# The same decoder-layer program, its instructions ordered by the builder's plain rule instead of its simulated timeline

## The chip, the cores and the metric

The kernel runs on one core of one Trainium2 chip. Its time is the device time of one execution in microseconds (us); the number to be predicted is the median over undisturbed runs. The core has five instruction queues that the kernel fills: PE (TensorE, matmuls), DVE (VectorE), ACT (ScalarE), POOL (GpSimd) and SP (SyncE), and each works its queue off in order; DMA transfers are issued from SP, ACT and POOL and run beside them.

## What is computed

One decoder layer over 512 tokens of width 1024, all in float32: a norm, one input projection, a gated short convolution and a gated linear recurrence over chunks of 32 tokens, an output projection with its residual, then a PEER feed-forward layer and a last norm. The time goes to PEER:

```python
def peer_ffn(x, wq, keys, u_tab, v_tab):
    ...
    q = (xt @ wq).reshape(t, PEER_HEADS, 2, HALF_Q)
    scores = jnp.einsum('thpd,hpnd->thpn', q, keys).astype(jnp.float32)
    s_top, i_top = lax.top_k(scores, PEER_TOPK)
    cand = (s_top[:, :, 0, :, None] + s_top[:, :, 1, None, :]).reshape(t, PEER_HEADS, PEER_TOPK * PEER_TOPK)
    c_score, c_idx = lax.top_k(cand, PEER_TOPK)
    ...
    expert = i1 * N_KEYS + i2
    gates = jax.nn.softmax(c_score, axis=-1)
    ...
        u = jnp.take(u_tab, eb, axis=0)
        a = jax.nn.gelu(jnp.einsum('td,thkd->thk', xb, u).astype(jnp.float32), approximate=False)
        w = (gb * a).astype(xb.dtype)
        vv = jnp.take(v_tab, eb, axis=0)
        return jnp.einsum('thk,thkd->td', w, vv)
```

For each token and each of 8 heads, 16 of 16,384 experts are selected (128 per token), each with a row of 1024 numbers in a u table and one in a v table.

## The kernel before

The 512 tokens are four blocks of 128. Blocks 1 to 3 (384 tokens) do the feed-forward layer **densely**: all 16,384 experts in 128 chunks of 128, with the gates as a matrix that is zero where an expert is not selected. Block 0 does it **sparsely**: it gathers its 128 rows of u and 128 rows of v for all its tokens, one 512 KB gather per selected rank, and multiplies on DVE. So PE and DVE share the layer.

The stages, in the order of the program:

1. The front, to about 260 us: projections, convolution, recurrence, output projection, the norm before PEER (which writes h2, transposed by L469). Every float32 operand is split in two parts, hi (a rounded copy that ACT makes, L99, whi) and lo (what remains, that DVE makes, L101, wlo), and `mm3` multiplies in three passes, hi x hi, hi x lo, lo x hi, which are lines L115, L116 and L117 of every dense matmul.
2. Queries and scores, to about 360 us.
3. The u stage, to about 795 us: `uchunk(c)` loads a 128x1024 raw tile of u (SP queue), splits it (whi, wlo), runs 24 matmuls 128x384 into `pa` (two PSUM buffers), and ACT takes the gelu out of it (`gl`, L447); the first 84 chunks spill gl to DRAM. Beside them DVE selects the experts: the top 16 of the scores (L518 to L523), the candidates and their top 16 (L554 to L586), the look-up of the indices (L595 to L607), block 0's experts (L613). Then 24 times `gate_m` builds, with four DVE operations on 128x2048 tiles A and B (L644 to L647), 32 small matmuls (L656, L657) and ACT evictions (`stg`, L659), a part of the dense gate matrix, which goes to DRAM. From 439 us on POOL issues the gathers of block 0 (`rows`, L675): `gu(j)` multiplies a gathered u row with h2 on DVE (L681), 16 of them are followed by a gelu and the gate (L685), and `gv(j)` adds a gathered v row times its weight to y0 (L689).
4. The v stage, from about 795 us to the end: for each of 128 chunks `vchunk` loads a raw tile of v, splits it, multiplies gl with the gates (w, L744), splits that (wh on ACT L747, wl on DVE L749), and 18 matmuls 128x512 are added up in `y` (six PSUM banks). The first 41 v chunks alternate with the last 41 u chunks. The remaining gathers go on beside them, at a pace of 2.65 per pair of chunks, later 1.1 per v chunk.
5. The last norm of each block (`finish`, L799 to L807) and the output.

Raw tiles and gathered rows come from **one ring** of buffers (8 in the u stage, 12 in the v stage, `raw_ring`). The next tenant of a buffer may be loaded when DVE has done with the former one: for a raw tile that is its wlo (L101), for a gathered row its product (L681 or L689). whi and wlo have four buffers each. POOL issues the gathers in order, each when its buffer is free.

```python
    def split(src):
        hi = ws.tile([P, D], F32R, tag="hi", name="whi")
        S.activation(hi, src, AF.Copy)
        lo = ws.tile([P, D], F32R, tag="lo", name="wlo")
        V.tensor_sub(lo, src, hi.bitcast(F32))
        return hi, lo
```
```python
    def rows(tab, j):
        t = ring[0]()
        G.indirect_dma_start(out=t, out_offset=None, in_=a[tab],
                             in_offset=bass.IndirectOffsetOnAxis(ap=e_i32[:, j:j + 1], axis=0))
```

What sets the order: the program is written stage by stage, with gates, chunks and gathers interleaved by the counts above. The builder (`tile.TileContext`) records all instructions and then puts them in an order of its own, queue by queue, that keeps the dependencies; while it does so it hands out the ring buffers, so that a tile's address, too, is a result of the order. Before, it does so with `schedule_with_timeline_sim=True`: it simulates a timeline and lets its times decide what comes next.

## Time and profile before

| | us |
|---|---|
| median of 2 runs | 1502.42 (1502.3 to 1502.54) |
| the profiled execution | 1500.03 |
| its span in the trace | 1498.1 |
| PE busy | 1462.3 (98%) |
| DVE busy | 1201.3 (80%) |
| ACT busy | 637.0 (43%) |
| POOL busy | 365.8 (24%) |
| mean granted clock of PE | 0.99 |

The span is the time from the first to the last instruction in the trace; 1.9 us of the profiled execution lie around it. "Granted clock" is the share of TensorE's full clock that it was allowed. All times in the rows below count from the start of the span.

### The profile page before, as it was taken

What the parts mean: (1) busy time and instruction counts of PE and PEld (TensorE: products, weight loads), DVE (VectorE), ACT (ScalarE), POOL (GpSimd) and SP (SyncE); (2) the same over time, 40 slices, a digit from 0 to 9 for tenths busy, and PEclk for the clock granted to TensorE, in tenths of its full rate; (3) what the DMA queues carried; (4) which work ended last, traced back from release to release, by engine and by line L of the source; (5) the groups of instructions that cost most, each with busy time, mean ns of one, the idle gap of its engine ahead of it and who ended that gap; (6) DMA issues with size and microseconds to landing.
All of it is one profiled execution on the core that took longest, in us unless ns stands there. A gap on an engine that the chain in (4) does not pass through costs nothing.

```text
span 1498.1 us, 21741 instructions
## 1 busy us (share of the span) xinstructions
PE 1462.3 (98%) x7929; PEld 1297.3 (87%) x7929; DVE 1201.3 (80%) x2312; ACT 637.0 (43%) x900; POOL 365.8 (24%) x284
## 2 busy tenths in 40 slices
PE   7999999999998999999999999999999999999997
PEld 6887777888998998889999999999998888888886
DVE  5847876799989988788829878778787788888887
ACT  5833324333443365666744333333333333333333
POOL 0000000000034142320014445444343224333340
PEclk9999999999999999999999999999999999999999
DMA  6231233622469789689779999998989999999993
GB/s 230 85 106 43 70 127 112 246 86 90 161 209 386 244 279 315 231 293 321 261 287 419 324 337 323 338 341 313 345 298 338 368 369 368 355 356 352 352 342 118
DMA packets 137770, 394.64 MB, mean 263 GB/s; under 512 B 13120, under 2 KB 59584, under 8 KB 135488
## 3 DMA queue, kind: packets, MB, share of 16 engines
q1 hardware_dynamic: 47520, 170.94, 31.5%
q0 software_dynamic: 39168, 159.40, 29.4%
q10 hardware_dynamic: 50976, 62.93, 11.9%
q8 instruction: 62, 1.02, 0.3%
q14 instruction: 44, 0.36, 0.1%
HBM read 346.82 MB, written 46.40 MB: 262 GB/s over the span
## 4 chain that ended last, share of the span: by engine, by line
PE 76%; DVE 6%; ACT 5%; issue 5%; DMA 5%; POOL 2%; ACTq 1%; POOLq 0%; DVEq 0%
PE y L116 10%; PE y L115 10%; PE y L117 10%; PE pa L115 8%; PE pa L116 7%; PE pa L117 7%; PE pm L115 7%; PE pm L116 6%; PE pm L117 6%; ACT stg L659 4%; DMA wraw<-in_v_dram,e_i 2%; POOL wraw L675 2%; DVE wlo L101 2%; DMA wraw<-in_u_dram,e_i 1%; PE pm L538 1%
## 5 line engine op out<-in xcount | busy, mean ns | idle before, releaser
L99 ACT ACTIVATE whi<-wraw 128x1024 fp32r<-128x1024 f32 x308 | 325.8, 1058 | 518.4 <-PE pa L116 205.4
L101 DVE TENSOR_TENSOR wlo<-wraw,whi 128x1024 fp32r<-128x1024 f32 x308 | 376.2, 1222 | 144.8 <-ACT whi L99 141.1
L115 PE MATMUL pa<-h2Thi,whi 128*128 128x384 f32 x1024 | 348.0, 340 | 12.7 <-ACT gl L447 12.4
L117 PE MATMUL pa<-h2Thi,wlo 128*128 128x384 f32 x1024 | 346.6, 338 | 0.0
L116 PE MATMUL pa<-h2Tlo,whi 128*128 128x384 f32 x1024 | 346.2, 338 | 0.0
L675 POOL DMA_INDIRECT wraw<-in_u_dram,e_i x128 | 183.3, 1432 | 490.2 <-DVE ci L523 178.6
L116 PE MATMUL y<-wlo,wh 128*128 128x512 f32 x768 | 299.5, 390 | 0.0
L115 PE MATMUL y<-whi,wh 128*128 128x512 f32 x768 | 298.9, 389 | 0.2 <-ACT wh L747 0.2
L117 PE MATMUL y<-whi,wl 128*128 128x512 f32 x768 | 296.8, 390 | 0.0
L675 POOL DMA_INDIRECT wraw<-in_v_dram,e_i x128 | 169.4, 1323 | 263.2 <-DVE wlo L101 122.0
L115 PEld LDWEIGHTS pa<-h2Thi,whi 128*128 128x128 f32 x1024 | 194.3, 190 | 17.8 <-ACT gl L447 15.9
L116 PEld LDWEIGHTS pa<-h2Tlo,whi 128*128 128x128 f32 x1024 | 194.4, 190 | 1.6
L117 PEld LDWEIGHTS pa<-h2Thi,wlo 128*128 128x128 f32 x1024 | 194.1, 190 | 0.0
L681 DVE SCALAR_TENSOR_TENSOR wraw<-wraw,h2n 128x1024 f32<-128x1024 f32 x128 | 155.9, 1219 | 34.7 <-DMA wraw<-in_u_dram,e_i 34.6
L689 DVE SCALAR_TENSOR_TENSOR y<-wraw,w,y 128x1024 f32<-128x1024 f32 x128 | 163.9, 1280 | 17.1 <-DMA wraw<-in_v_dram,e_i 16.9
L117 PEld LDWEIGHTS y<-whi,wl 128*128 128x128 f32 x768 | 144.1, 188 | 30.2
L115 PEld LDWEIGHTS y<-whi,wh 128*128 128x128 f32 x768 | 144.2, 188 | 29.7 <-ACT wh L747 0.6
L116 PEld LDWEIGHTS y<-wlo,wh 128*128 128x128 f32 x768 | 144.1, 188 | 29.0
L747 ACT ACTIVATE wh<-w 128x384 fp32r<-128x384 f32 x128 | 65.8, 522 | 208.2 <-PE y L116 97.6
L659 ACT ACTIVATE stg<-pm 128x512 f32<-128x512 f32 x96 | 92.3, 1156 | 17.7 <-PE pm L657 17.7
L749 DVE TENSOR_TENSOR wl<-w,wh 128x384 fp32r<-128x384 f32 x128 | 70.2, 554 | 22.8 <-ACT wh L747 22.3
L115 PE MATMUL pm<-hThi,whi 128*128 128x512 f32 x192 | 77.7, 406 | 8.4 <-ACT whi L99 8.4
(240 smaller groups left out, 1694.7 us busy)
## 6 DMA issues: line engine op xcount, KB each, us to landing
wraw<-in_u_l_dram SPq DMA_DIRECT2D x128, 512.0 KB, 5.6
wraw<-in_v_l_dram SPq DMA_DIRECT2D x128, 512.0 KB, 6.4
Gd<-stg ACTq DMA_DIRECT2D x12, 2048.0 KB, 7.6
Gt<-Gd POOLq DMA_DIRECT2D x16, 1536.0 KB, 9.7
Ad<-gl ACTq DMA_DIRECT2D x84, 192.0 KB, 5.0
glr<-Ad ACTq DMA_DIRECT2D x84, 192.0 KB, 5.2
wraw<-in_w_in_dram SPq DMA_DIRECT2D x24, 512.0 KB, 3.7
wraw<-in_wq_dram SPq DMA_DIRECT2D x16, 512.0 KB, 7.4
```

What stands on the lines that cost most here:

```text
L99: S.activation(hi, src, AF.Copy)
L101: V.tensor_sub(lo, src, hi.bitcast(F32))
L115: PE.matmul(out, l[0], r[0], start=first, stop=False)
L116: PE.matmul(out, l[0], r[1], start=False, stop=False)
L117: PE.matmul(out, l[1], r[0], start=False, stop=last)
L538: PE.matmul(o[:, tb * NK:(tb + 1) * NK], q[:, tb * P:(tb + 1) * P], keys[:, i, :], start=True, stop=True)
L659: S.activation(st[:, t0:t0 + 4, :], o3, AF.Copy, scale=1.0 / GSC)
L675: G.indirect_dma_start(out=t, out_offset=None, in_=a[tab], in_offset=bass.IndirectOffsetOnAxis(ap=e_i32[:, j:j + 1], axis=0))
L681: V.scalar_tensor_tensor(r, r, 1.0, h2n, op0=OP.mult, op1=OP.mult, accum_out=act0[:, j:j + 1])
L689: V.scalar_tensor_tensor(y0, r, w0[:, j:j + 1], y0, op0=OP.mult, op1=OP.add)
L747: S.activation(wh, w, AF.Copy)
L749: V.tensor_sub(wl, w, wh.bitcast(F32))
```

## The change

One word in one line: the builder is told not to simulate a timeline, and orders the instructions by its plain rule.

```diff
-    with tile.TileContext(nc, schedule_with_timeline_sim=True) as tc, ExitStack() as ctx:
+    with tile.TileContext(nc, schedule_with_timeline_sim=False) as tc, ExitStack() as ctx:
```

The kernel's functions are untouched, and the instructions are the same (ACT's table loads apart, of which there are 19 instead of 21, since they depend on the order). What moves is shown at three places.

**DVE, u stage, at the first splits beside the selection.** In the names, wlo_3443, wlo_3477, wlo_3754 and wlo_3788 are the lo parts of four u chunks that follow one another; tv, ti, mr, cand, cv and ci belong to the selection. Before (19 rows of selection stand between the first two, 20 between the second and the third, 18 between the third and the fourth):

```order
L101 TENSOR_TENSOR wlo_3443<-wraw_3439,whi_3441 128x1024
L518 MAX tv1_2185<-s_3147 128x8
...
L523 MAX_INDEX ti3_2191<-tv3_2187,mr_3163 128x8
L101 TENSOR_TENSOR wlo_3477<-wraw_3473,whi_3475 128x1024
...
L522 MAX tv2_2186<-mr_3188 128x8
L101 TENSOR_TENSOR wlo_3754<-wraw_3750,whi_3752 128x1024
...
L558 TENSOR_TENSOR cand_3508<-tv1_2185 128x8x8
L101 TENSOR_TENSOR wlo_3788<-wraw_3784,whi_3786 128x1024
```

Of the change, the same stretch:

```order
L101 TENSOR_TENSOR wlo_3443<-wraw_3439,whi_3441 128x1024
L518 MAX tv1_2185<-s_3147 128x8
...
L522 MAX cv_3213<-mr_3259 128x8
L101 TENSOR_TENSOR wlo_3477<-wraw_3473,whi_3475 128x1024
...
L521 MATCH_REPLACE mr_3694<-cv_3648,cand_3640 128x50
L101 TENSOR_TENSOR wlo_3754<-wraw_3750,whi_3752 128x1024
L522 MAX cv_3648<-mr_3694 128x8
L101 TENSOR_TENSOR wlo_3788<-wraw_3784,whi_3786 128x1024
```

Now 87 rows stand between the first two and 197 between the second and the third (a row may stand for a few instructions of one form), and one between the third and the fourth. The selection moved ahead of wlo_3754.

**PE at the same place.** pa_3479 is the chunk of wlo_3477, pa_3756 that of wlo_3754, pa_3790 the next. Of the change, from the end of pa_3479 on (before, the first L117 of pa_3756 follows its first L115 and L116, and pa_3790 comes after it):

```order
L117 MATMUL pa_3479<-h2Thi_1870,wlo_3477 128x384
L115 MATMUL pa_3756<-h2Thi_1870,whi_3752 128x384
L116 MATMUL pa_3756<-h2Tlo_1871,whi_3752 128x384
L115 MATMUL pa_3790<-h2Thi_1870,whi_3786 128x384
L116 MATMUL pa_3790<-h2Tlo_1871,whi_3786 128x384
L117 MATMUL pa_3756<-h2Thi_1870,wlo_3754 128x384
```

Two matmuls of pa_3790 moved ahead; between the last matmul of the chunk before and the first that needs wlo_3754, four stand.

**DVE, v stage, around a gather.** wraw_11856 and wraw_11891 are gathered rows; the wlo are splits of raw tiles (wraw_11469 and so on); w and wl belong to v chunks. Before, from the product of the gathered row wraw_11821, which frees the buffer that wraw_11926 gets, to the product of that:

```order
L681 SCALAR_TENSOR_TENSOR wraw_11821,act0_2160<-wraw_11821,h2n_2162 128x1024
L749 TENSOR_TENSOR wl_11621<-w_11617,wh_11619 128x384
L744 TENSOR_TENSOR w_11760<-glr_11752,Gt_11215 128x384
L101 TENSOR_TENSOR wlo_11615<-wraw_11611,whi_11613 128x1024
L689 SCALAR_TENSOR_TENSOR y0_2163<-wraw_11856,w0_2161,y0_2163 128x1024
L749 TENSOR_TENSOR wl_11656<-w_11652,wh_11654 128x384
L101 TENSOR_TENSOR wlo_11650<-wraw_11646,whi_11648 128x1024
L681 SCALAR_TENSOR_TENSOR wraw_11891,act0_2160<-wraw_11891,h2n_2162 128x1024
L749 TENSOR_TENSOR wl_11694<-w_11690,wh_11692 128x384
L101 TENSOR_TENSOR wlo_11688<-wraw_11684,whi_11686 128x1024
L689 SCALAR_TENSOR_TENSOR y0_2163<-wraw_11926,w0_2161,y0_2163 128x1024
```

Of the change, from the split of wraw_11469, which frees the buffer that wraw_11856 gets:

```order
L101 TENSOR_TENSOR wlo_11473<-wraw_11469,whi_11471 128x1024
L681 SCALAR_TENSOR_TENSOR wraw_11821,act0_2160<-wraw_11821,h2n_2162 128x1024
L749 TENSOR_TENSOR wl_11516<-w_11512,wh_11514 128x384
L744 TENSOR_TENSOR w_11652<-glr_11644,Gt_11215 128x384
L101 TENSOR_TENSOR wlo_11510<-wraw_11506,whi_11508 128x1024
L689 SCALAR_TENSOR_TENSOR y0_2163<-wraw_11856,w0_2161,y0_2163 128x1024
L749 TENSOR_TENSOR wl_11551<-w_11547,wh_11549 128x384
L744 TENSOR_TENSOR w_11690<-glr_11682,Gt_11215 128x384
L101 TENSOR_TENSOR wlo_11545<-wraw_11541,whi_11543 128x1024
L681 SCALAR_TENSOR_TENSOR wraw_11891,act0_2160<-wraw_11891,h2n_2162 128x1024
```

The gathers moved about three chunks ahead against the splits, and each took over another buffer, as the addresses of the two built programs tell:

| gathered row | former tenant before | splits from its end to the use | former tenant in the change | splits from its end to the use |
|---|---|---|---|---|
| wraw_11821 | wraw_11714 | 3 | wraw_11434 | 1 |
| wraw_11856 | wraw_11749 | 4 | wraw_11469 | 1 |
| wraw_11891 | wraw_11784 | 3 | wraw_11506 | 1 |
| wraw_11926 | wraw_11821 | 3 | wraw_11541 | 1 |
| wraw_11961 | wraw_11856 | 3 | wraw_11576 | 1 |

Over the last 176 gathers (numbers 80 to 255) the splits from the freeing to the use are 1 for 10, 2 for 49, 3 for 67, 4 for 40 and 5 for 10 of them before; in the change 1 for 153, 2 for 22 and 3 for one.

In the u stage, besides, the 32 matmuls of a gate now stand together behind two chunks instead of among the matmuls of a chunk, six products of gathered rows (L681) stand in a row on DVE ahead of one of the first gates, and ACT's gl and stg copies stand there behind a whi. The three last `finish` stand one after another instead of interleaved.

## Rows read from the trace of the kernel before

**Rows 1.** The page's first table: busy time, share of the span, instructions.
```profile
PE 1462.3 (98%) x7929; PEld 1297.3 (87%) x7929; DVE 1201.3 (80%) x2312; ACT 637.0 (43%) x900; POOL 365.8 (24%) x284
```

**Rows 2.** A window: length, busy PE, PEld, DVE, ACT, POOL; clock; DMA share; GB/s.
```profile
1150.00:1200.00 50.00, 50.00 (x222) 41.42 (x221) 40.14 (x57) 17.64 (x25) 14.46 (x15) 1.00 0.98 366
```

**Rows 3.** Waits of PE: us in total, times, longest.
```profile
PE pa L115 <- ACT gl L447: 12.4, 8, 4.2
```

**Rows 4.** Windows as in rows 2, at two waits of PE.
```profile
455.00:460.00 5.00, 3.73 (x12) 3.73 (x13) 5.00 (x15) 1.70 (x3) 2.72 (x3) 0.50 0.98 349
...
590.00:595.00 5.00, 3.21 (x21) 2.89 (x21) 5.00 (x6) 1.44 (x2) 0.00 (x0) 1.00 1.06 388
```

**Rows 5.** PE's timeline there: start, length, instruction, idle before and its releaser.
```profile
456.27 0.69 PE L115 MATMUL pa<-h2Thi,whi 128*128 128x384 f32 x1 [4.17 <-ACT gl L447]
456.76 0.52 PE L116 MATMUL pa<-h2Tlo,whi 128*128 128x384 f32 x1
457.08 0.52 PE L117 MATMUL pa<-h2Thi,wlo 128*128 128x384 f32 x1
...
461.24 0.40 PE L115 MATMUL pa<-h2Thi,whi 128*128 128x384 f32 x1
...
593.51 0.40 PE L656 MATMUL pm<-B,A 128*128 128x128 f16 x4 [1.79 <-DVE B L646]
```

**Rows 6.** ACT's timeline, u stage: hi parts, released by finished chunks.
```profile
381.24 1.06 ACT L99 ACTIVATE whi<-wraw 128x1024 fp32r<-128x1024 f32 x1 [2.72 <-PE pa L116]
...
385.39 1.06 ACT L99 ACTIVATE whi<-wraw 128x1024 fp32r<-128x1024 f32 x1 [2.72 <-PE pa L116]
```

**Rows 7.** DVE's timeline at two of the splits (wlo_3443 and wlo_3754).
```profile
363.82 1.23 DVE L101 TENSOR_TENSOR wlo<-wraw,whi 128x1024 fp32r<-128x1024 f32 x1 [0.44 <-ACT whi L99]
...
374.54 1.21 DVE L101 TENSOR_TENSOR wlo<-wraw,whi 128x1024 fp32r<-128x1024 f32 x1
```

**Rows 8.** One window, DVE busy: all; L101 alone; L681 alone.
```profile
363.82:447.80 83.98, 79.52 (x435) 1.00 0.53 173
...
363.82:447.80 83.98, 21.82 (x18) 1.00 0.53 173
...
363.82:447.80 83.98, 7.33 (x12) 1.00 0.53 173
```

**Rows 9.** A window of PE alone: the u stage.
```profile
430.00:800.00 370.00, 355.19 (x2504) 0.98 0.84 295
```

**Rows 10.** Instruction groups of DVE: busy us, mean ns, idle before and releasers.
```profile
L101 DVE TENSOR_TENSOR wlo<-wraw,whi 128x1024 fp32r<-128x1024 f32 x308 | 376.2, 1222 | 144.8 <-ACT whi L99 141.1 <-PE pm L538 2.4
...
L689 DVE SCALAR_TENSOR_TENSOR y<-wraw,w,y 128x1024 f32<-128x1024 f32 x128 | 163.9, 1280 | 17.1 <-DMA wraw<-in_v_dram,e_i 16.9
...
L749 DVE TENSOR_TENSOR wl<-w,wh 128x384 fp32r<-128x384 f32 x128 | 70.2, 554 | 22.8 <-ACT wh L747 22.3
...
L744 DVE TENSOR_TENSOR w<-glr,Gt 128x384 f32<-128x384 f32 x84 | 43.0, 552 | 8.4 <-issue 5.3 <-DMA Gt<-Gd 2.8
```

**Rows 11.** Timelines of DVE and POOL: a buffer freed, the gather issued.
```profile
1013.90 1.23 DVE L101 TENSOR_TENSOR wlo<-wraw,whi 128x1024 fp32r<-128x1024 f32 x1 [2.32 <-ACT whi L99]
...
1015.40 1.01 POOL L675 DMA_INDIRECT wraw<-in_v_dram,e_i  x1 [3.00 <-DVE wlo L101]
```

**Rows 12.** The gathers' line (L675) by stretch: 550 to 750, 1130 to 1450.
```profile
DMA to landing us min/median/max: 4.9/5.9/12.6
...
DMA to landing us min/median/max: 4.5/7.3/13.9
```

**Rows 13.** The first of them as a window of POOL: busy, clock, DMA share, GB/s.
```profile
550.00:750.00 200.00, 41.66 (x18) 0.98 0.81 281
```

**Rows 14.** Waits of DVE from 795 to 1450 us.
```profile
DVE y L689 <- DMA wraw<-in_v_dram,e_i: 11.2, 13, 2.6
DVE wraw L681 <- DMA wraw<-in_u_dram,e_i: 10.4, 9, 2.5
```

**Rows 15.** DVE's timeline: its last instruction.
```profile
1493.52 1.41 DVE L806 SCALAR_TENSOR_TENSOR wraw<-wraw,vo,nfb 128x512 f32<-128x512 f32 x2
```

## The prediction

> **What bounds the kernel now.** I read the page's first table, the waits of the TensorE queue (PE), its busy time by stretches of 50 us, then the timelines where PE did wait. PE is busy for 1462.3 of 1498.1 us [rows 1]; VectorE (DVE), next, for 1201.3. From about 800 us, when the chunks of the v table run, a 50-us window is full: 50.00 us of PE, 41.42 in weight loads, DVE about 41 [rows 2]. So any order with the same instructions can gain at most the 36 us in which PE is idle, and loses every microsecond that it makes PE wait. The largest part of the idle time, 12.4 us, are eight waits of u chunks for the PSUM buffer that ACT's gelu frees [rows 3].
>
> PE's clock has a price of its own here. After the wait of 4.17 us that ended at 456.27 the window 455 to 460 ran at 0.50 (1.2 instead of 2.4 GHz); after the 1.79 us that ended at 593.51 the clock stayed 1.00 [rows 4, 5]. In the slow stretch a 384-column matmul starts every 0.32 us (456.76, 457.08) [rows 5]; at full clock a chunk's 24 take 4.15 us, 0.17 each [rows 6]. Over the 5 us from 456.27 to 461.24 that costs about 2.4, with its ends 3 us.
>
> **The change part by part.** No instruction is added or taken away apart from two table loads of ACT; the order in every queue changes, and with it which ring buffer each raw tile gets. I go through the program by stages. The first 360 us stand almost as they stood: 0 to +4, I take 0.
>
> *Selection ahead of the splits (360 to 450 us).* PE runs a u chunk each 4.15 us (381.24 to 385.39, the releases of ACT's whi by finished chunks) [rows 6]. Each needs a wlo from DVE. Before, DVE made wlo_3443 at 363.82, the one after next (wlo_3754) at 374.54 [rows 7], with a share of the selection between. Now all the selection instructions that the order shows between wlo_3443 and wlo_3754, 286 of them, come first. Their cost: DVE's busy time from 363.82 to 447.80 is 79.52; 21.82 of it are the splits and 7.33 six products of gathered rows, so selection is 79.52 - 21.82 - 7.33 = 50.4 us, nearly all of it now ahead of wlo_3754 [rows 8]. That split then ends at 363.8 + 1.2 + 50.4 + 2 x 1.2 = 417.8. Its chunk started at 385.4 before; two first matmuls of it and two of the next are all that PE has meanwhile. **+32 us** of idle PE, then half clock: **+3**. The order puts the next splits (wlo_3788, wlo_3822) right behind, so this is paid once. Nothing pays it back: PE has no slack later, and DVE's lead, gained by having selected early, is not what PE lacks. Bounds: 0, if the selection were spread after all, which the order excludes short of a wrong reading; 35, if all of it and the clock are paid.
>
> *Gates (430 to 800 us).* PE is busy 355.19 of these 370 us, so 14.8 idle plus some 6 of half clock are there to win [rows 9]. Against it, the 32 matmuls of a gate now stand together behind two chunks, and before one of the first gates stand six products of gathered rows on DVE, 7.3 us [rows 8] that PE waits for with its chunk splits behind it; ACT's gelu copies also stand behind a whi that waits for a gather's buffer. I take one such stall of 7.3 with its 3 of clock more than before: **+10**, bounds -15 (all of the idle time goes) and +20 (two).
>
> *The ring in the v stage (800 to 1450 us).* This is the largest term. A gather on POOL needs a ring buffer, which is free when DVE has done with its last tenant, and DVE waits in order for the landed rows. Before, 2 to 4 weight splits lie between the freeing and the use in three quarters of the cases; now just one in 153 of the last 176 gathers. Follow the rows of the change: wlo_11473 frees the buffer of wraw_11856; one split later DVE stands at its product and must wait until it is issued and landed; behind it come wl, w and the next wlo, which frees the next buffer but one. So two splits take R + 3.6 us, where R is from freeing to landing, and 3.6 is 1.28 + 0.55 + 0.55 + 1.22 [rows 10]. From freeing to issue takes 0.3 (a split ends at 1013.90 + 1.23 = 1015.13, POOL issues at 1015.40) [rows 11]. Landing is not one number: median 7.3 us from 1130 to 1450, where a window has 366 GB/s, and 5.9 from 550 to 750, at 281 GB/s [rows 2, 12, 13]. With slower chunks traffic thins: 366 x 4.1 / 4.9 is 306 GB/s, nearest to the second, so I take 5.9. R = 6.2, a split each (6.2 + 3.6) / 2 = 4.9 us against PE's 4.1 (18 matmuls; 222 in 50 us, some records missing [rows 2]). 0.8 x 169 splits (41 u and 128 v chunks) = 135; 23 of 176 gathers have a longer window, so 0.87 x 135: **+115**. Bounds: with the least landing shown, 4.5 [rows 12], it is (4.8 + 3.6) / 2 = 4.2, so +0 to 15; with 7.3 it is 5.6 and 1.5 x 169 = +250. DVE waited for landed rows only 11.2 + 10.4 us here before [rows 14]; covered by four split buffers, PE saw nothing of it.
>
> The Trainium skill, DMA: Bandwidth & Descriptors, section on the SWDGE path of one DMA, gives a fixed 2.0 us plus bytes over 436 GB/s for a transfer issued by GpSimd. For these 512 KB an estimate by it is 3.2 us, R = 3.5, a split each 3.6 us: PE would not wait and this term would be nothing (the first rival's 1550). The trace disagrees, with 4.5 as its least and 7.3 as its median.
>
> *Tail.* The three last norms stand one after another now; DVE's last instruction starts at 1493.52 and takes 1.41 [rows 15]; two more of these behind each other: **+3**, bounds 0 and 6.
>
> Sum on the profiled run of 1500.0: 1500 + 32 + 3 + 10 + 115 + 3 = 1663. The median of the runs shown is 2.4 above the profiled run (1502.42 against 1500.03), which gives **1665 us**.
>
> **The rivals.**
>
> *The gathers land in time.* As chunks slow down, landings fall to the least shown and the ring is no bound: 1665 - 115 = 1550. For it: traffic in the v stage is what lengthens the landings, and a ring that is waited for thins it. Against it: even at 281 GB/s the median is 5.9. It decides where R + 3.6 is under 2 x 4.1, a landing of 4.3.
>
> *The clock falls in the v stage too.* If the waits there bunch up to 3 us and more (landings reach 13.9 [rows 12]), each is followed by about 3 us lost. One such wait in every second of the 85 pairs of splits adds 42 x 3 = 126, in every pair 250: 1791 to 1915, say 1850. For it: a wait of 4.17 cost the clock. Against it: the mean wait is 1.6 per pair, and 1.79 did not [rows 4, 5]. The Trainium skill, TensorE: Matmul & The Clock Gate, in its section on HAM oscillation, tells of a kernel whose every step waits for a transfer and so starts each step at the low clock; the trace agrees for single long waits (0.50 after 4.17 us) and shows no such series.
>
> *Not slower.* The plain rule keeps PE's own queue dense and the waits of [rows 3] vanish: 12.4, 1.8 at the gate [rows 5] and 6 of clock, so 1502 - 20 = 1482. That holds if the selection block hides behind work of PE and the landings are 4.3 or less. For it: PE's matmuls are the same and its order is tighter. Against it: between the last matmul of one chunk and the first needing wlo_3754 only four matmuls, 0.7 us, stand. It ends on this side once that wait is under 20 us and the ring costs nothing.
>
> **How the numbers follow.** As forecast, with the ring at 4.7 to 5.6 a split: 0.70, own range 1600 to 1800. Gathers in time, about 1550: 0.12. Clock in the v stage, 1,800 and more: 0.13. Not slower: 0.05, 0.02 of it under 1472, the other 0.03 within 2%. The range 1545 to 1800 holds the first two, 0.82. About 2%, 30 us, is what a measurement of this kernel tells from no change: under 1472 faster (0.02), 1472 to 1532 the same (0.03), above it slower (0.95).
>
> **What would show it.** A PE wait of 30 us near 387 to 418, released by wlo of L101, then a clock of 0.50. In the v stage, waits of DVE's L681 and L689 for gathers of 100 us and more in sum, in place of 21.6; waits of PE's pa and y for wlo of about the sum forecast; splits 4.9 us apart; traffic near 306 GB/s; a landing near 5.9. No such wait near 400 would make the first term wrong. PE full after 800 would make the third wrong, by the landing if that is under 4.5, and by the reading of the ring if it isn't. A granted clock well under 1.00 there would speak for the second rival.

## The result, and the profile after

The median is 1731.99 us (1730.73 to 1733.25, two runs) against 1502.42: a ratio of 1.1531, 95% interval 1.1504 to 1.1559. The profiled execution has a span of 1729.0 us, 230.9 more than before, at a mean granted clock of 0.957.

The first table of the page after, columns as in [rows 1]:

```profile
PE 1519.1 (88%) x7929; PEld 1321.9 (76%) x7929; DVE 1209.1 (70%) x2312; ACT 626.6 (36%) x898; POOL 359.8 (21%) x284
```

The instructions are the same but for two table loads of ACT, and so, almost, is the busy time, except PE's, which rose by 57 us, as it ran longer at the lower clock (a mean of 0.957 instead of 0.99). The other 174 of the 231 us are idle time of PE: no engine is over 90% busy now. The waits of PE tell what it waits for, in the columns of [rows 3]:

```profile
PE y L116 <- DVE wlo L101: 110.1, 58, 4.7
PE pa L117 <- DVE wlo L101: 66.3, 18, 30.1
PE pm L115 <- ACT whi L99: 7.5, 1, 7.5
PE pa L115 <- ACT gl L447: 4.7, 3, 2.2
```

The waits for gl of [rows 3] are down from 12.4 us to 4.7; in their place stand 176 us of waiting for wlo, the split that DVE makes, one of them 30.1 long. Three times that can be read off both traces, the starts of the first v matmul, of the 42nd wh (where the u chunks end) and of the last v matmul, place the loss (worked out by counting the instructions):

| | first v matmul | 42nd wh | last v matmul | span |
|---|---|---|---|---|
| before | 792.6 | 1118.3 | 1488.4 | 1498.1 |
| after | 844.2 | 1259.6 | 1720.3 | 1729.0 |
| stage longer by | 51.6 | 89.7 | 90.6 | -1.0 (the tail) |

**The selection.** The timelines of PE and DVE at the long wait, and PE's windows around it:

```profile
413.38 0.69 PE L117 MATMUL pa<-h2Thi,wlo 128*128 128x384 f32 x1 [30.13 <-DVE wlo L101]
```
```profile
412.11 1.21 DVE L101 TENSOR_TENSOR wlo<-wraw,whi 128x1024 fp32r<-128x1024 f32 x1
```
```profile
385.00:413.00 28.00, 0.00 (x0) 0.00 (x0) 28.00 (x229) 0.62 (x2) 0.00 (x0) 0.50 0.00 1
413.00:418.00 5.00, 4.62 (x14) 4.63 (x15) 5.00 (x18) 0.31 (x1) 0.00 (x0) 0.50 0.62 202
418.00:423.00 5.00, 5.00 (x27) 5.00 (x27) 5.00 (x23) 2.84 (x3) 0.00 (x0) 0.87 0.29 113
```

For 28 us DVE is full with 229 instructions, all of them selection but the last, which is the split, and PE does nothing; then PE goes on at 0.50.

**The v stage.** DVE's waits from 844 to 1720 us:

```profile
DVE wraw L681 <- DMA wraw<-in_u_dram,e_i: 146.8, 63, 5.3
DVE y L689 <- DMA wraw<-in_v_dram,e_i: 98.1, 53, 5.9
DVE w L744 <- issue: 28.4, 9, 6.7
DVE w L744 <- DMA Gt<-Gd: 11.4, 5, 3.7
```

The waits for landed rows were 21.6 us in sum [rows 14] and are 244.9 now. One turn of the ring on the timelines of DVE and POOL:

```profile
1320.79 1.22 DVE L101 TENSOR_TENSOR wlo<-wraw,whi 128x1024 fp32r<-128x1024 f32 x1
...
1324.07 1.22 DVE L101 TENSOR_TENSOR wlo<-wraw,whi 128x1024 fp32r<-128x1024 f32 x1
...
1328.46 1.23 DVE L681 SCALAR_TENSOR_TENSOR wraw<-wraw,h2n 128x1024 f32<-128x1024 f32 x1 [2.71 <-DMA wraw<-in_u_dram,e_i]
...
1330.68 1.22 DVE L101 TENSOR_TENSOR wlo<-wraw,whi 128x1024 fp32r<-128x1024 f32 x1
```
```profile
1322.29 1.01 POOL L675 DMA_INDIRECT wraw<-in_u_dram,e_i  x1 [4.43 <-DVE wlo L101]
```

The split that ends at 1322.01 frees a buffer; POOL issues the gather at 1322.29; one split later DVE wants its rows and stands until 1328.46, 6.45 us after the freeing; the second split after the first ends at 1331.90, 9.9 us after it. The gathers' line (L675) from 844 to 1260 and from 1260 to 1600, and one window for both stages (columns of [rows 2]):

```profile
DMA to landing us min/median/max: 4.2/5.6/10.9
...
DMA to landing us min/median/max: 4.0/5.9/10.0
```
```profile
844.00:1720.00 876.00, 748.21 (x3265) 619.73 (x3264) 575.34 (x754) 244.42 (x356) 256.31 (x212) 0.96 0.75 265
```

The gathers land sooner than before (a median of 7.3 us from 1130 to 1450 [rows 12]), so slower gathers are not the cause.

### The profile page after: what moved, and what is told of

Its sections match the earlier page's. It is cut to its first block, busy times and chain, and to the rows that moved or that the text cites. A ratio compares the mean times of both kernels' runs of the same rounds, so it can differ in the third digit from the quotient of the medians.

```text
span 1729.0 us, 21788 instructions
## 1 busy us (share of the span) xinstructions
PE 1519.1 (88%) x7929; PEld 1321.9 (76%) x7929; DVE 1209.1 (70%) x2312; ACT 626.6 (36%) x898; POOL 359.8 (21%) x284
## 5 line engine op out<-in xcount | busy, mean ns | idle before, releaser
L101 DVE TENSOR_TENSOR wlo<-wraw,whi 128x1024 fp32r<-128x1024 f32 x308 | 374.1, 1220 | 76.4 <-ACT whi L99 74.8
L116 PE MATMUL y<-wlo,wh 128*128 128x512 f32 x768 | 319.4, 416 | 110.2 <-DVE wlo L101 110.1
L99 ACT ACTIVATE whi<-wraw 128x1024 fp32r<-128x1024 f32 x308 | 317.9, 1051 | 264.6 <-PE pm L116 101.5
L117 PE MATMUL pa<-h2Thi,wlo 128*128 128x384 f32 x1024 | 352.2, 344 | 66.4 <-DVE wlo L101 66.3
L115 PE MATMUL pa<-h2Thi,whi 128*128 128x384 f32 x1024 | 352.4, 344 | 5.7 <-ACT gl L447 4.7
L116 PE MATMUL pa<-h2Tlo,whi 128*128 128x384 f32 x1024 | 349.3, 341 | 1.4 <-DVE h2Tlo L473 1.4
L675 POOL DMA_INDIRECT wraw<-in_u_dram,e_i x128 | 184.0, 1437 | 656.5 <-DVE wlo L101 462.7
L117 PE MATMUL y<-whi,wl 128*128 128x512 f32 x768 | 312.4, 407 | 3.5 <-DVE wl L749 3.3
L115 PE MATMUL y<-whi,wh 128*128 128x512 f32 x768 | 311.7, 406 | 1.0 <-ACT whi L99 0.6
L681 DVE SCALAR_TENSOR_TENSOR wraw<-wraw,h2n 128x1024 f32<-128x1024 f32 x128 | 156.3, 1224 | 195.0 <-DMA wraw<-in_u_dram,e_i 194.7
L116 PEld LDWEIGHTS y<-wlo,wh 128*128 128x128 f32 x768 | 152.1, 198 | 166.5 <-DVE wlo L101 135.5
L117 PEld LDWEIGHTS pa<-h2Thi,wlo 128*128 128x128 f32 x1024 | 197.7, 193 | 72.8 <-DVE wlo L101 72.7
L689 DVE SCALAR_TENSOR_TENSOR y<-wraw,w,y 128x1024 f32<-128x1024 f32 x128 | 164.2, 1282 | 124.9 <-DMA wraw<-in_v_dram,e_i 124.5
L675 POOL DMA_INDIRECT wraw<-in_v_dram,e_i x128 | 162.8, 1272 | 355.2 <-DVE wlo L101 196.3
L115 PEld LDWEIGHTS pa<-h2Thi,whi 128*128 128x128 f32 x1024 | 197.8, 193 | 8.7 <-ACT gl L447 6.0
L116 PEld LDWEIGHTS pa<-h2Tlo,whi 128*128 128x128 f32 x1024 | 197.6, 193 | 3.2 <-DVE h2Tlo L473 1.6
L117 PEld LDWEIGHTS y<-whi,wl 128*128 128x128 f32 x768 | 152.0, 198 | 35.3 <-DVE wl L749 4.6
L115 PEld LDWEIGHTS y<-whi,wh 128*128 128x128 f32 x768 | 151.5, 197 | 34.1 <-ACT whi L99 1.2
L447 ACT ACTIVATE gl<-pa 128x384 f32<-128x384 f32 x128 | 61.1, 477 | 66.0 <-PE pa L117 65.1
L115 PE MATMUL pm<-hThi,whi 128*128 128x512 f32 x192 | 77.8, 405 | 7.5 <-ACT whi L99 7.5
```

Source lines behind the costliest of these rows:

```text
L115: PE.matmul(out, l[0], r[0], start=first, stop=False)
L116: PE.matmul(out, l[0], r[1], start=False, stop=False)
L117: PE.matmul(out, l[1], r[0], start=False, stop=last)
L447: S.activation(gl, o, AF.Gelu)
L675: G.indirect_dma_start(out=t, out_offset=None, in_=a[tab], in_offset=bass.IndirectOffsetOnAxis(ap=e_i32[:, j:j + 1], axis=0))
L681: V.scalar_tensor_tensor(r, r, 1.0, h2n, op0=OP.mult, op1=OP.mult, accum_out=act0[:, j:j + 1])
```

## The experiments

The theory: in the v stage the pace is set by DVE waiting for gathers whose buffers come free one split too late; in the u stage by selection that stands ahead of a split. The rivals: TensorE's half clock after its waits; the gates' loads (Gt), whose waits of 39.8 us the forecast hadn't counted; a ring that is just too small; DVE having too much to do in any order. The runs were made in four groups, each on a chip of its own, and in each the kernel before was run beside them and took 1501 to 1503 us. Times of different groups are compared across chips. Some edits move the lines below them by a few: L682 and L684 are the product L681, L690 and L692 the product L689, and so on. The table has the three starts of above for each kernel, in the order in which they are told:

| kernel | order by | time | first v matmul | 42nd wh | last v matmul |
|---|---|---|---|---|---|
| two rings of 6, v stage | plain rule | 1573.5 | 845.9 | 1185.4 | 1562.7 |
| third pass cut to a quarter | plain rule | 1740.7 | 843.1 | 1262.3 | 1730.3 |
| gates loaded from SP | plain rule | 1742.2 | 842.1 | 1265.5 | 1729.8 |
| u chunks ahead of selection | plain rule | 1725.3 | 820.5 | 1245.2 | 1715.7 |
| two rings of 6, chunks first | plain rule | 1551.8 | 823.8 | 1165.4 | 1543.2 |
| one ring of 16 | plain rule | 1741.2 | 844.3 | 1259.1 | 1726.3 |
| two rings, 8 and 4 | plain rule | 1629.4 | 849.7 | 1242.7 | 1622.7 |
| rings cut in both stages, chunks first | plain rule | 1535.2 | 806.5 | 1147.3 | 1524.1 |
| the same, gates from SP | plain rule | 1529.4 | 806.1 | 1140.4 | 1520.6 |
| rings cut in both stages | simulation | 1524.5 | 779.3 | 1102.1 | 1512.9 |
| rings cut in both stages, gates from SP | simulation | 1531.6 | 783.3 | 1106.1 | 1519.9 |
| ring of the u stage cut | simulation | 1491.2 | 784.1 | 1108.7 | 1480.7 |

### Two rings in the v stage

```diff
+    gring = []
...
-        t = ring[0]()
+        t = (gring or ring)[0]()
...
-    raw_ring(sb("rm", 1), MRING)
+    rm = sb("rm", 1)
+    raw_ring(rm, 6)
+    gring.append(lambda: rm.tile([P, D], F32, tag="rows", name="wraw", bufs=6))
```

> The plain rule is kept; in the v stage the ring of 12 buffers is cut in two, 6 for raw tiles and 6 for gathered rows. The splits that stand between the freeing of a gather's buffer and its use go from 1 (153 of the last 176) to 3 (126), 2 (33) or more. Theory (turnaround of a gather's buffer sets the pace of the v stage): DVE's waits for landed rows after 844 us fall from 146.8 + 98.1 = 245 us to under 50, splits come 4.1 to 4.4 us apart, and the time falls from 1732 to 1560 to 1610. Rival (the v stage is long because TensorE runs at half clock after its waits, or because transfers are slower in this order): the time stays above 1680.

1573.5 us (ratio to before 1.0473, interval 1.0396 to 1.0549). The same 12 buffers, the same rule, and 158 us of the 230 are gone. DVE's waits for landed rows after 844 us, of two rings:

```profile
DVE y L690 <- DMA wraw<-in_v_dram,e_i: 1.2, 3, 0.4
DVE wraw L682 <- DMA wraw<-in_u_dram,e_i: 0.4, 1, 0.4
```

1.6 us in place of 244.9, and the v stage takes 716.8 us in place of 876.1 (695.8 before). The theory holds; the stage up to the first v matmul is untouched.

### A third of PE's work in the v stage cut to a quarter

```diff
-            mm3(yp[tb][hf], (wh[:, ts_], wl[:, ts_]), (vh[:, cs], vl[:, cs]), first, last)
+            o = yp[tb][hf]
+            PE.matmul(o, wh[:, ts_], vh[:, cs], start=first, stop=False)
+            PE.matmul(o, wh[:, ts_], vl[:, cs], start=False, stop=False)
+            PE.matmul(o[:, :P], wl[:, ts_], vh[:, hf * T:hf * T + P], start=False, stop=last)
```

> The plain rule is kept. The third of the three passes of each v matmul (L117) multiplies only 128 of its 512 columns, so a part of the product is left out; the order of all queues and the buffers are those of the changed kernel. PE has some 768 x 0.15 = 115 us less to do. Theory (DVE and the gathers set the pace, and the 78 us that PE spends at half clock in the v stage lie inside waits that it has anyway): 1732 within 15 us, with PE idle for about 100 us more. Rival (half clock after the waits is on the path, and made of the 180 us that the v stage grew the 53 by which PE's busy time rose): 1680 or less.

1740.7 us. The same window as the last of the section before, of this kernel:

```profile
844.00:1720.00 876.00, 695.84 (x3208) 586.44 (x3206) 566.51 (x731) 239.99 (x344) 256.69 (x212) 0.90 0.76 264
```

PE is busy for 52 us less, runs at 0.90 instead of 0.96, and the kernel is no faster. So PE isn't what sets the pace of the v stage, and its half clock there, 78 us in 21 pieces in the changed kernel, lies inside waits that it has anyway: it makes PE busier, not the kernel longer. The rival falls.

### The gates' loads from another queue

```diff
-        G.dma_start(out=Gt[g].rearrange("p b c t -> p (b c t)"), in_=Gd[g].rearrange("p b c t -> p (b c t)"))
+        nc.sync.dma_start(out=Gt[g].rearrange("p b c t -> p (b c t)"), in_=Gd[g].rearrange("p b c t -> p (b c t)"))
```

> The plain rule is kept; the 16 loads of the gates (Gt) are issued from SP instead of POOL, where they stand behind gathers that wait for buffers. The windows of the gathers stay as in the changed kernel (1 split for 158 of 176). Theory (waiting for the gates is a second term of its own in the v stage, 28.4 + 11.4 = 39.8 us of DVE against 8.1 before): about 30 us less, 1700. Rival (the ring is the only bound, and what is saved here is waited for at the next gather): 1724 to 1740.

1742.2 us: no gain. DVE's waits from 840 to 1720 us:

```profile
DVE wraw L681 <- DMA wraw<-in_u_dram,e_i: 151.0, 61, 5.9
DVE y L689 <- DMA wraw<-in_v_dram,e_i: 145.8, 69, 6.7
```

The waits for the gates are gone from the list, and those for landed rows have grown from 244.9 to 296.8, by more than the 39.8 that went. A gather whose buffer comes free one split ahead has its 6 to 7 us to go, and what DVE waited for meanwhile was part of it. Here the theory that I put down was wrong, and the rival right: these 39.8 us were no term of their own.

### u chunks written ahead of the selection

```diff
     for cost, f, args in work:
-        f(*args)
         done += cost
         while nu < (SPILL - UOFF) * done / total:
             uchunk(nu)
             nu += 1
+        f(*args)
```

> The plain rule is kept; in the program the u chunks that were written behind each piece of selection or gate work are written ahead of it. The longest run of DVE instructions between two splits falls from 199 to 51. Theory (the wait of 30.1 us for one split is the selection standing in front of it): that wait goes, and with it its half clock, 1732 - 33 = 1699. Rival (DVE has too much to do between 360 and 450 us in any order, and PE waits later for what it doesn't wait for here): 1732 within 10.

1725.3 us, 7 less, not 33. The wait of 30.1 is gone: in the changed kernel PE waited for wlo eight times from 360 to 844 us, 53.2 us in all, 30.1 of them at once. PE's waits from 360 to 820 us, of this kernel:

```profile
PE pa L117 <- DVE wlo L101: 19.8, 5, 8.8
PE pm L626 <- DVE ix L607: 13.3, 2, 9.1
```

13.3 us came back as waits of the gates for the looked-up indices, which the selection now gives later, and the v stage began 23.7 us earlier, not 33. Then the v stage, with the same windows of the ring, took 895.2 instead of 876.1 us and gave most of that back. The mean from the freeing to the use of gathers 80 to 255, worked out by matching each gather with its buffer's former tenant, is 7.02 us here and 6.85 in the changed kernel; by the pair formula 0.17 is worth 14 us of these 19. Why they were slower by that much is open.

### Both edits

Two rings of 6 in the v stage and the chunks ahead of the selection.

> The plain rule with both edits of before together: two rings of 6 in the v stage, and the u chunks written ahead of the selection. The chunks-first kernel reached the v stage 24 us earlier (820.5 instead of 844.2) and gave 19 of them back there, where the gathers set the pace. Theory (the 24 us are real, and were lost only in a stage whose length hangs on the gathers' landing): with two rings they stay, 1573.5 - 24 = 1550. Rival (work that was pushed out of the selection has to be done later anyway): 1565 or more.

1551.8 us, 21.7 less than with two rings alone, as the theory had it: once the gathers' landing doesn't set the pace, the earlier start is kept.

### A larger ring

```diff
-MRING = 12
+MRING = 16
```

> The plain rule, with one ring of 16 buffers instead of 12 in the v stage. The splits between the freeing of a gather's buffer and its use remain 1 for 146 of the last 176 gathers, since raw tiles, loaded further ahead, take the new buffers. Theory (what counts is those splits, not the number of buffers): 1732 within 20. Rival (the ring is too small for the plain rule): 1690 or less.

1741.2 us. A third more buffers in one ring bring nothing: under the plain rule raw tiles, loaded further ahead, take them. By the addresses of the built programs, the splits from the freeing of a raw tile's buffer to its own split rise from 9.3 to 12.9 in the mean over the last 165 raw tiles, while the gathers keep their one.

### Rings of 8 and 4

The edit of the first experiment with 8 and 4 for 6 and 6.

> The plain rule with two rings in the v stage, 8 buffers for raw tiles and 4 for gathered rows: 2 splits between the freeing and the use for 146 of 176 gathers, where the rings of 6 and 6 have 3. Theory: with 2, three splits take 6.9 (mean from freeing to use in the changed kernel) + 3.6 = 10.5 us, 3.5 each, which is under PE's 4.1, so the pace is PE's again and the time that of the rings of 6 and 6, 1573 within 20. Rival (every split in between is worth a part of the loss): about half of the gain, 1630 to 1660.

1629.4 us, in the range of the rival. DVE waits for landed rows again, from 844 to 1620 us, for 65.7 us instead of the 1.6 with rings of 6:

```profile
DVE y L690 <- DMA wraw<-in_v_dram,e_i: 39.2, 42, 2.5
...
DVE wraw L682 <- DMA wraw<-in_u_dram,e_i: 26.5, 24, 2.3
```

The theory had too few products between the splits. DVE's busy time in the pair stage (850 to 1243 us), of L690, of L682 and of L101 alone:

```profile
850.00:1243.00 393.00, 104.05 (x82) 0.97 0.94 338
...
850.00:1243.00 393.00, 100.22 (x164) 0.97 0.94 338
...
850.00:1243.00 393.00, 93.81 (x77) 0.97 0.94 338
```

82 + 82 products (each L682 has a second instruction that reads its sum) for 77 splits, 2.1 a split; in the changed kernel from 844 to 1260 us they are 56 + 56 for 78, 1.4. With a ring of their own the gathers run ahead of the pace that the program sets (with rings of 6 there are 83 + 83 of them in 339 us), and my 3.6 us between two uses had one product a split in it. Nearly all of the loss against two rings of 6 is in this stage (393 us, not 339.5); the stage behind it takes 380 against 377.

### The u stage's ring cut in two as well

```diff
-    raw_ring(sel.enter_context(tc.tile_pool(name="rs", bufs=1)), 8)
+    rs = sel.enter_context(tc.tile_pool(name="rs", bufs=1))
+    raw_ring(rs, 5)
+    gring.append(lambda: rs.tile([P, D], F32, tag="rows", name="wraw", bufs=3))
...
-    gring.append(lambda: rm.tile([P, D], F32, tag="rows", name="wraw", bufs=6))
+    gring.insert(0, lambda: rm.tile([P, D], F32, tag="rows", name="wraw", bufs=6))
```

> As the kernel with two rings of 6 and chunks first, and the ring of 8 of the u stage is cut in two as well, 5 for raw tiles and 3 for gathered rows. Theory (a part of what the u stage lost, 53 us against the kernel of before, is waiting for gathers that share their ring with raw tiles; DVE waited for landed rows for 74 us there): 10 to 20 us less than with one ring of 8, 1530 to 1540. Rival (the u stage loses to DVE's order alone): 1550 within 5.

1535.2 us, 16.6 less, as the theory had it. DVE's waits for landed rows in the u stage (450 to 806 us, of this kernel, then 450 to 820 of the one with one ring of 8):

```profile
DVE wraw L684 <- DMA wraw<-in_u_dram,e_i: 23.8, 10, 8.0
...
DVE y L692 <- DMA wraw<-in_v_dram,e_i: 7.7, 5, 3.6
```
```profile
DVE y L690 <- DMA wraw<-in_v_dram,e_i: 34.0, 10, 8.1
DVE wraw L682 <- DMA wraw<-in_u_dram,e_i: 30.2, 9, 8.1
```

31.5 instead of 64.2 us. And PE's waits for wlo in u chunks, of this kernel, then of the one with one ring of 8:

```profile
PE pa L118 <- DVE wlo L101: 2.2, 3, 1.5
```
```profile
PE pa L118 <- DVE wlo L101: 19.3, 7, 9.0
```

These 17.1 us are about what was gained: the ring had a share in the u stage's loss too. (The 53 and 74 us of the expectation are those of kernels without chunks first; with chunks first it was 31 us and these 64.2.) With three edits the plain rule is within 2.3% of the simulated one (interval 1.7 to 3.0%).

### The gates' loads again, without the ring's bound

The last kernel with the edit that issues the gates' loads from SP.

> The kernel with both rings cut in two and chunks first (1535.2 us), and the loads of the gates issued from SP instead of POOL. DVE waits 53.8 us for the gates in the kernel with two rings of 6 and chunks first, since POOL issues a gate load behind gathers. Theory (what the ring hid in the changed kernel comes out once the ring no longer sets the pace): PE's 18 us of idle time in the v stage go, 1518 to 1526. Rival (the gates are no term, as moving them brought nothing in the changed kernel): 1535 within 4.

1529.4 us, 5.8 less (two runs each, of different groups; 3.5 between the two profiled runs). In these the v stage's first part gained 6.5 us (334.3 instead of 340.8) and the rest gave 3 back. DVE's waits for the gates from 800 to 1500 us, of this kernel, then of the last one:

```profile
DVE w L749 <- DMA Gt<-Gd: 31.3, 12, 6.1
```
```profile
DVE w L749 <- DMA Gt<-Gd: 49.5, 14, 7.7
```

So the gates' loads are a small term of their own when the gathers don't hide it, less than the 9 to 17 expected. What they cost in full isn't shown, since from SP, too, DVE waits 31.3 us for them. The 28 us that remain against the kernel before were not followed up.

### The simulated order with its rings cut

Both rings cut, chunks where they were, and the order by simulation as before; the second kernel has 4 and 4 buffers in the u stage and the gates' loads on SP.

> The simulated timeline as in the kernel before, with the ring of 8 cut in 5 for raw tiles and 3 for gathered rows and the ring of 12 in 6 and 6. Theory (the simulated order already keeps 2 to 4 splits between, so in the v stage, where PE is full, nothing is to be had): 1500 within 8. Rival (the 12.4 us of waits for the gelu's copies in the u stage, with 6 of half clock, come from whi copies that wait for gathers' buffers): 1482 to 1490, faster than both kernels.

> As the last, with 4 and 4 buffers in the u stage, and the loads of the gates issued from SP. Theory: 1500 within 8, as the v stage is full of PE work in any case. Rival (as for the last): 1482 to 1490.

1524.5 us (1.0155, 1.0126 to 1.0184) and 1531.6 (1.0203, 1.0171 to 1.0235): 1.6% and 2.0% slower than before, which neither theory had. The u stage did gain: the first v matmul stands at 779.3 and 783.3, 13 and 9 us earlier than before. Among the last 87 v chunks they lost 41 and 44 us. PE's waits there, and ACT's and DVE's timelines at one of the seven, of the first of the two kernels:

```profile
PE y L116 <- ACT wh L752: 24.1, 7, 3.5
```
```profile
1166.32 1.06 ACT L99 ACTIVATE whi<-wraw 128x1024 fp32r<-128x1024 f32 x1 [3.01 <-PE y L118]
1170.35 1.06 ACT L99 ACTIVATE whi<-wraw 128x1024 fp32r<-128x1024 f32 x1 [2.97 <-PE y L118]
1173.16 0.52 ACT L752 ACTIVATE wh<-w 128x384 fp32r<-128x384 f32 x1 [1.76 <-DVE w L749]
```
```profile
1171.44 1.23 DVE L101 TENSOR_TENSOR wlo<-wraw,whi 128x1024 fp32r<-128x1024 f32 x1 [2.80 <-ACT whi L99]
1172.58 1.96 DVE L749 TENSOR_TENSOR w<-glr,Gt 128x384 f32<-128x384 f32 x4
```

With 6 raw buffers the simulated order has four w in a row behind a wlo here; that waits for whi, that for a finished chunk, and PE has no wh left. PE's granted clock is 0.50 for 27.3 us in seven pieces, one by each wait, and half of that, 13.7 us, is an estimate of what it costs; with the waits it makes 37.8 of the 41. Here, where PE sets the pace, the low clock is paid, and in the changed kernel it wasn't. The same cut that mends the plain order makes the simulated one worse there.

### The simulated order with only the u stage's ring cut

The cut of the u stage's ring alone, with its second ring given up where the v stage begins:

```diff
     raw_ring(sb("rm", 1), MRING)
+    gring.clear()
```

> The simulated timeline and the single ring of 12 in the v stage, both as in the kernel before; only the ring of 8 of the u stage is cut in 5 buffers for raw tiles and 3 for gathered rows. With the cut in both stages the simulated order reached its first v matmul at 779.3 us instead of 792.6, without half clock in the u stage, but lost 41 us among the last 87 v chunks, where PE waited seven times 3.4 us for wh. Theory (the first comes from the ring of the u stage, the second from the 6 raw buffers of the v stage): 13 us less than before, 1486 to 1490, faster than both kernels. Rival (the earlier start is taken back by the v stage whatever its ring): 1500 within 4.

1491.2 us over six runs against 1503.5 over eleven of before on the same chip: 0.9922, interval 0.9900 to 0.9943, a little above the expected 1486 to 1490, and faster than both kernels, 0.8% faster than the one before. PE's waits of this kernel:

```profile
PE pa L116 <- ACT gl L448: 10.6, 6, 4.1
PE pm L116 <- ACT whi L99: 8.4, 1, 8.4
PE pm L470 <- DVE h2s L463: 3.1, 1, 3.1
PE y L116 <- ACT wh L751: 0.9, 1, 0.9
```

The first v matmul stands at 784.1, 8.5 us earlier than before and not 13, and the v stage keeps it; the waits for wh are down to 0.9, so it was by the cut in the v stage that the simulated order lost. The waits for gl are still 10.6 us (12.4 before), so most of the gain isn't those: PE's idle time from 360 us to the first v matmul fell from 14.8 to 10.6 us and its half clock from 13.7 to 10.2 us, by counting; together that is about 6 of the 8.5. The rest is open.

## Why the prediction was right, point by point

**The bound.** Right: PE was full and had 36 us to win; the new order made it idle for 174 us more. The one kernel here that won anything, the simulated order with the ring of the u stage cut, won 12.

**The first 360 us, 0.** Wrong by a little: the gelu of the chunk just ahead of the block stands at 382.1 instead of 386.4, 4.3 us earlier, where 0 to +4 was forecast.

**The selection, +32 and +3.** Right in place, cause and size: a wait of 30.13 us for wlo at 413.38, half clock behind it, and the chunk's gelu 31.9 us later than before (422.4 against 390.5), which with the lead of 4.3 is 36 us. The bound of zero was excluded by the order, as said. "Nothing pays it back" holds as far as shown: the later u stage lost more still. What an order without the block can win is less than the wait: 24 us (the u chunks written ahead of the selection), since the gates then wait for the look-up.

**The gates, +10.** Right in sign, too small: from that chunk to the first v matmul it was 51.6 - 31.9 = 19.7 us. I named ACT's gelu copies behind whi, and these waits fell, to 4.7 us. What grew was DVE waiting for landed rows, 74.4 us from 450 to 844 us against 25.4 from 450 to 793 before, and PE for wlo behind them (21.8 us from 423 us on, none before):

```profile
DVE wraw L681 <- DMA wraw<-in_u_dram,e_i: 47.9, 18, 7.9
...
DVE y L689 <- DMA wraw<-in_v_dram,e_i: 26.5, 10, 6.3
```

With chunks first, cutting the u stage's ring took 16.6 us away. So the ring, which the forecast let begin at 800 us, is most likely the cause here too; in the changed kernel itself that cut was not tried.

**The ring, +115.** The mechanism is shown: the turn can be read in one place of the timeline; two rings take 158 us away; more buffers in one ring take nothing; less work for PE takes nothing. The size was 89.7 + 90.6 = 180.3 us, 65 more than forecast; the stage's 876 us are 5.2 a split, not 4.9. The landing was forecast well (5.9; 5.6 and 5.9 measured), so was the median from freeing to use (6.2; 6.6 for gathers 80 to 175 and 6.2 for the rest). What was mis-sized is R, put together from typical values: waits add up by their means. Matched gather by gather, R is 6.85 us in the mean for gathers 80 to 255. Of these, 0.44 us are from freeing to issue (0.3 forecast) and 6.04 from issue to landing (5.9 forecast); for 0.37 us the landed row waits for DVE, which is mostly busy with a split then, and that part was left out. The 0.65 are worth 55 us by the pair formula, 31 of them the last part. From the use to the end of the next split it was 3.43 and not 3.6, worth 14 us the other way. That (6.85 + 3.43) / 2 x 169 = 869 us are nearly the stage's 876 is bookkeeping and no test, since one span begins where the other ends. Taking 13% off for longer windows, 20 us, wasn't borne out either: without it 135 + 55 - 14 = 176 us come close to the 180; why the longer windows saved nothing was not tested. Traffic was 265 GB/s, not 306.

**The tail, +3.** Wrong, with no weight: from the last v matmul to the end 8.7 us after, 9.7 before.

**The rivals.** The gathers did not land in time. The transfer formula of the Trainium skill, DMA: Bandwidth & Descriptors, section on the SWDGE path of one DMA, would have had 3.2 us by estimate, and the least of these landings was 4.0; the trace disagrees. The clock did fall in the v stage, 21 times, which I gave as a rival with a price of up to 250 us, and the price was nothing (the third pass cut): I had added it to a stage that PE no longer sets. The section on HAM oscillation in the Trainium skill, TensorE: Matmul & The Clock Gate, describes such a series, each step waiting for a transfer and starting at the low clock; the falls are in this trace (0.96 over the stage, 0.90 in the window from 1050 to 1100), its cost isn't, since here DVE and not PE closes the loop. The rival on the other side failed at both of its conditions.

**The sum.** 1665 against 1732: the 67 us missing are 65 of the ring, 10 of the gates and 1 of the selection, less 4 of the first 360 us, 4 of the tail and 1 between profiled run and median. That the small errors cancel is luck; the ring's stands.

**What it overlooked.** The gates' loads behind waiting gathers on POOL (39.8 us of DVE's waits). Taking them off POOL won nothing while the gathers set the pace, and 4 to 6 us once they didn't.

## What to carry to other kernels

When a change only reorders, look in the new order for the places where something must go round: from the instruction that frees a buffer over the transfer to the instruction that waits for it. Count what stands between, and put the mean time from freeing to use, not the transfer's median, against it. Where one ring serves two kinds of tiles, look at which kind takes the buffers: under the plain rule it was the one that is loaded ahead, with 12 and with 16 buffers, and a ring of its own gave the other its distance. Waits on such a loop hide others (a gate's load, a low clock): they are not terms until the loop is cut. And a cut belongs to an order: what won 158 us under the plain rule lost 41 in the simulated order's v stage.

## What the runs showed of the hardware

TensorE's granted clock stood at 0.50 in a window in which the engine did nothing at all (385 to 413 us) and remained there as it began again, to about 419. A low clock can be free: with three quarters of the third pass cut, PE's clock in the v stage fell from 0.96 to 0.90 and the time did not change beyond 9 us. It is not free where PE sets the pace: 27.3 us at 0.50 were some 14 of the 41 us that the simulated order lost with its v ring cut. A gather of 512 KB issued from POOL took at least 4.0 us in the v stage of the changed kernel (844 to 1600 us), and its median was 5.6 to 5.9 at 259 to 281 GB/s of traffic against 7.3 where a window had 366 GB/s [rows 2, 12]: with other transfers as they are in this kernel, waiting for it thins the traffic, and shortens the landing by only a fifth.
